# Gate and up weight sums of a seven-product FFN: subtractions on VectorE, or accumulating DMAs from DRAM

## The chip, the core and the metric

The kernel runs on one core of one Trainium2 chip. The metric is the device time of one execution in microseconds (us). The engines named below are PE (TensorE, matrix multiply), DVE (VectorE), ACT (ScalarE), POOL (GpSimd) and SP (SyncE, which here only issues DMAs). Each engine works through its own instructions in a fixed order, and an instruction that waits for a semaphore holds up everything behind it on the same engine.

## What is computed

A two-layer encoder trunk on 512 positions of width 1024, in float32. Layer 0 mixes by a gated linear recurrence (RG-LRU), layer 1 by stick-breaking attention; after each mixer comes a SwiGLU feed-forward block (FFN) with inner width 2816, and a last RMSNorm ends it.

```python
D_MODEL, SEQ, DEPTH, D_FF = 1024, 512, 2, 2816

def _swiglu(h, w_gate, w_up, w_down):
    g = h @ w_gate
    u = h @ w_up
    return (jax.nn.silu(g) * u) @ w_down

for layer in range(DEPTH):
    h = _rmsnorm(x, norm_mix_g[layer])
    x = x + (_rglru_mixer(h, ...) if layer % 2 == 0 else _sb_mixer(h, ...))
    h = _rmsnorm(x, norm_ffn_g[layer])
    x = x + _swiglu(h, ffn_w_gate[layer], ffn_w_up[layer], ffn_w_down[layer])
return _rmsnorm(x, final_g)
```

The change concerns the products with `w_gate` and `w_up` only (and the signs around them).

## The kernel before

**Float32 by three products.** Every weight block of 128x1024 floats is loaded by SP into an SBUF tile, then split: ACT casts it to a reduced float type (`wh`, line L236), and DVE or POOL subtracts that from the original to get the rest (`wl`, L237). PE multiplies high by high, low by high and high by low. One such loaded and split block is a "chunk". The method `chunk()` hands out chunks in the fixed order of the list made by `plan()`; in the FFN it keeps the splits three chunks ahead of PE and the loads up to eight ahead. In the FFN the split tiles have four buffers in turn (three `wh`/`wl`, and `wh4`/`wl4` for every fourth chunk), so the split of a chunk can begin only when PE is done with the chunk four places before it. Loads that go to `raw` tiles have four buffers.

**Seven products in place of eight.** In the FFN, the two halves of the positions and gate and up together form a 2x2 block product (rows: first and second 256 positions; columns: gate and up; the inner dimension cut in two halves of 512). It is done by a Strassen-Winograd scheme with seven block products, called q = 1 to 7 in the code. For this, the weights of one unit of 512 inner columns (units u = 0 to 4, two pieces c = 0, 1 for each product; unit 5 has 256 columns and one piece) come as four blocks: b0 (gate, first half of the inner dimension), b1 (up, first half), b2 (gate, second half), b3 (up, second half). The products take b0, b2 and b3 as they are, and four sums: q5 takes b1 - b0, q6 takes b3 - b1 + b0, q4 takes b2 - b3 + b1 - b0, and q7 takes b3 - b1.

**Where the sums are made.** The class `Piece` stands for one product's piece in the chunk list. `Piece.load()` issues the load of one block on SP (b0 and b2 into `raw` tiles, b1 and b3 into tiles `b1`, `b3` with two buffers each). `Piece.source()` is called when the chunk is split, and makes the sum by a DVE subtraction of 128x1024 floats (L76): into a tile `tt` for q5, in place for q6 and q4, and into b1's tile for q7. That is four subtractions for a piece, 11 pieces in a layer, so 88 in all.

**The order.** Unit 0 runs its products as 1, 2, 5, 6, 3, 7, 4, with no other chunk between them; its first four chunks (q1 and q2, both pieces) are loaded before the FFN begins, and its tiles for b1 and b3 lie in memory that the mixer before it holds until PE has done its last product. Units 1 to 5 run 1, 5, 6, 3, 7, 2, 4, with the down-projection's chunks (24 matmuls each, `down_pair`) of the unit before in between: in unit 1 the first of them stands behind q3, in later units behind q5. PE's order is written by hand; the order on the other engines is set by a scheduler that gives the splits a high priority. The splits of the down-projection's chunks put `wl` on POOL, those of the seven products on DVE. What PE leaves in its banks is added up by ACT copies (L684, L705, L712) and DVE additions (L689, L715, L723).

`ffn_in()` makes the seven products' left operands while the mixer's output projection still runs.

Of the kernel before, what the change touches and what calls it, by code (L numbers as in the profile page):

```python
# [52 lines left out]


class Piece:
    LOADS = {1: 0, 5: 1, 6: 3, 2: 2}
# [4 lines left out]
    def load(self):
        un, kern = self.unit, self.unit.kern
        n = self.LOADS.get(self.q)
        if n is None:
# [7 lines left out]
        kern.nc.sync.dma_start(t, un.src[n * un.np + self.c])

    def source(self):
        un, kern, q, c = self.unit, self.unit.kern, self.q, self.c
        sub = lambda o, x, y: kern.nc.vector.tensor_tensor(o, x, y, ALU.subtract)  # L76
        b = lambda n: un.b[n, c]
        if q == 1:
            return b(0)
        if q == 2:  # L80
            return b(2)
        if q == 3:
            return b(3)
# [12 lines left out]


class Kern:
# [232 lines left out]
    def ffn_in(self, m, g):  # L331
        nc = self.nc
        lo, hi = slice(0, HS), slice(HS, S)
        sub = lambda o, x, y: nc.vector.tensor_tensor(o, x, y, ALU.subtract)
# [7 lines left out]
        if m < 4:  # L342
            ua, w2 = self.tmp(), self.tmp()
            t, t3 = self.new("a11", F32R, first=True), self.new("s3", F32R, first=True)
# [266 lines left out]
    def ffn(self, l, gnext):  # L611
        nc, tc = self.nc, self.tc
        mm = nc.tensor.matmul
        with tc.tile_pool(name=f"ffn{l}", bufs=1) as self.fp, tc.manual_schedule(engines={mybir.EngineType.PE}):
# [50 lines left out]
                    mm(out, lhsT=w[1][:, ws], rhs=h[:, cs], start=False, stop=en, skip_group_check=True)  # L665

            def add(m, bank):
                nc.vector.tensor_tensor(self.x[m], self.x[m], bank, ALU.add)  # L668
# [511 lines left out]
```

## Time and profile before

| | |
|---|---|
| three timed runs | 1150.55, 1150.94, 1151.56 us (median 1150.94) |
| profiled execution, span from first to last instruction | 1150.0 us (its time beyond the span is not given apart) |
| PE busy | 1120.0 us, 97% of the span |
| DVE, ACT, POOL busy | 816.6, 647.0 and 298.3 us |
| mean granted TensorE clock | 0.990 of full speed |
| DMA | 114.23 MB, queue of SP 30.9% of 16 DMA engines' span |
| first FFN, PE's first product | 166.92 us from the start of the span |
| second FFN, PE's first product | 786.05 us |

How to read it: PE is busy nearly throughout, so an edit changes the time only where it lengthens or shortens a wait of PE, or PE's own work. The busy time of the other engines counts only through the moment at which they hand something to PE. Rows of the timeline show the start in us from the span's start, the duration, the engine, the line, and the tiles written and read; the bracket at a row's end is the idle time before it and what ended it.

### The profile page before, as it was taken

How to read it: one execution, taken by the hardware profiler on the slowest of the kernel's cores; microseconds unless marked ns; L12 is line 12 of the kernel's file. 1: busy time of each engine (PE TensorE's matmuls, PEld its weight loads, DVE VectorE, ACT ScalarE, POOL GpSimd, SP SyncE). 2: the span in 40 equal slices, each digit the busy share in tenths (PEclk: the TensorE clock that was granted, in tenths of full speed). 3: DMA queues.
4: the chain of work that ended last, by engine and by line, in shares of the span. 5: the costliest groups of instructions: out<-in, count | busy, mean ns of one | idle time of the engine just before them, and what ended most of it. 6: DMA issues, size and time to landing. Idle time of an engine off the chain costs nothing. (4 is left out here: it accounts for less than half of the span.)

```text
span 1150.0 us, 14308 instructions
## 1 busy us (share of the span) xinstructions
PE 1120.0 (97%) x5363; PEld 931.0 (81%) x5363; DVE 816.6 (71%) x1080; ACT 647.0 (56%) x967; POOL 298.3 (26%) x167
## 2 busy tenths in 40 slices
PE   8999999999999999999999999899999999999995
PEld 6887788888888888988888888778788888888884
DVE  7878889767574757473488888679967575765655
ACT  6598576634353444453489999767544434343442
POOL 2451333020111111272054444314011111101231
PEclk9999999999999999999999999899999999999997
DMA  7222234332424222122434334033432331322201
GB/s 241 91 90 91 96 105 169 96 114 79 134 74 134 68 92 92 58 89 94 118 95 117 92 90 108 25 109 111 147 128 92 95 120 61 117 84 92 74 19 74
DMA packets 35862, 114.23 MB, mean 99 GB/s; under 512 B 4560, under 2 KB 5584, under 8 KB 35792
## 3 DMA queue, kind: packets, MB, share of 16 engines
q1 hardware_dynamic: 35504, 112.66, 30.9%
q8 instruction: 42, 0.69, 0.2%
q10 hardware_dynamic: 288, 0.66, 0.2%
q14 instruction: 28, 0.23, 0.1%
HBM read 102.81 MB, written 2.10 MB: 91 GB/s over the span
## 5 line engine op out<-in xcount | busy, mean ns | idle before, releaser
L237 POOL TENSOR_TENSOR wl<-raw,wh 128x1024 fp32r<-128x1024 f32 (+1 forms) x74 | 177.9, 2405 | 642.2 <-ACT wh L236 638.5
L236 ACT CAST wh<-raw 128x1024 fp32r<-128x1024 f32 (+1 forms) x154 | 155.9, 1016 | 186.1 <-PE bank L644 88.2
L642 PE MATMUL bank<-wh,ow 128*128 128x512 f32 (+1 forms) x480 | 179.4, 374 | 3.6 <-DVE st L389 3.6
L644 PE MATMUL bank<-wh,ow 128*128 128x512 f32 (+1 forms) x480 | 178.3, 372 | 0.0
L643 PE MATMUL bank<-wl,ow 128*128 128x512 f32 (+1 forms) x480 | 178.3, 371 | 0.0
L237 DVE TENSOR_TENSOR wl<-raw,wh 128x1024 fp32r<-128x1024 f32 (+1 forms) x80 | 98.5, 1234 | 46.0 <-ACT wh L236 45.1
L236 ACT CAST wh<-tt 128x1024 fp32r<-128x1024 f32 x66 | 69.4, 1052 | 109.5 <-PE bank L664 55.1
L663 PE MATMUL bank<-hh,wh 128*128 128x512 f32 (+1 forms) x324 | 125.4, 387 | 0.0
L664 PE MATMUL bank<-hl,wh 128*128 128x512 f32 (+1 forms) x324 | 125.3, 387 | 0.0
L665 PE MATMUL bank<-hh,wl 128*128 128x512 f32 (+1 forms) x324 | 125.2, 387 | 0.0
L668 DVE TENSOR_TENSOR x<-x,bank 128x512 f32<-128x512 f32 x87 | 59.6, 685 | 85.2 <-PE bank L665 84.3
L642 PEld LDWEIGHTS bank<-wh,ow 128*128 128x128 f32 x480 | 90.4, 188 | 19.7 <-ACT wh L236 4.4
L237 DVE TENSOR_TENSOR wl<-tt,wh 128x1024 fp32r<-128x1024 f32 x66 | 80.6, 1222 | 34.9 <-ACT wh L236 34.5
L270 PE MATMUL bank<-uh,wh 128*128 128x512 f32 x256 | 102.4, 400 | 1.8 <-ACT wh L236 1.2
L644 PEld LDWEIGHTS bank<-wh,ow 128*128 128x128 f32 x480 | 90.4, 188 | 15.7
L643 PEld LDWEIGHTS bank<-wl,ow 128*128 128x128 f32 x480 | 90.5, 188 | 15.3
L272 PE MATMUL bank<-uh,wl 128*128 128x512 f32 x256 | 100.3, 392 | 1.4 <-DVE wl L237 1.4
L271 PE MATMUL bank<-ul,wh 128*128 128x512 f32 x256 | 99.7, 390 | 0.3 <-DVE ul L326 0.3
L237 DVE TENSOR_TENSOR wl<-b,wh 128x1024 fp32r<-128x1024 f32 x44 | 54.8, 1246 | 51.8 <-ACT wh L236 51.6
L236 ACT CAST wh<-b 128x1024 fp32r<-128x1024 f32 x44 | 46.3, 1053 | 62.1 <-PE bank L644 26.7
L665 PEld LDWEIGHTS bank<-hh,wl 128*128 128x128 f32 x324 | 60.8, 188 | 12.4
L663 PEld LDWEIGHTS bank<-hh,wh 128*128 128x128 f32 x324 | 60.9, 188 | 12.1
(219 smaller groups left out, 2422.3 us busy)
## 6 DMA issues: line engine op xcount, KB each, us to landing
raw<-w_gu SPq DMA_DIRECT2D x44, 512.0 KB, 3.5
b<-w_gu SPq DMA_DIRECT2D x44, 512.0 KB, 3.9
raw<-w_dn SPq DMA_DIRECT2D x44, 512.0 KB, 3.5
raw<-w_qk SPq DMA_DIRECT2D x16, 512.0 KB, 3.4
raw<-w_in SPq DMA_DIRECT2D x14, 512.0 KB, 3.7
raw<-w_ao SPq DMA_DIRECT2D x8, 512.0 KB, 3.8
raw<-w_v SPq DMA_DIRECT2D x8, 512.0 KB, 3.5
qh<-qx SPq DMA_DIRECT2D x32, 128.0 KB, 2.4
```

Of the source, the lines that this page charges most:

```text
L236: self.nc.scalar.copy(wh[:, c], raw[:, c])
L237: self.wl_engine(i).tensor_tensor(wl[:, c], raw[:, c], wh[:, c].bitcast(F32), ALU.subtract)
L270: mm(out, lhsT=wh, rhs=xh, start=first, stop=False)
L271: mm(out, lhsT=wh, rhs=xl, start=False, stop=False)
L272: mm(out, lhsT=wl, rhs=xh, start=False, stop=last)
L642: mm(out[j][:, :w], lhsT=oh[:, ts(j)], rhs=wh[:, ws], start=st, stop=False, skip_group_check=True)
L643: mm(out[j][:, :w], lhsT=oh[:, ts(j)], rhs=wl[:, ws], start=False, stop=False, skip_group_check=True)
L644: mm(out[j][:, :w], lhsT=ol[:, ts(j)], rhs=wh[:, ws], start=False, stop=en, skip_group_check=True)
L663: mm(out, lhsT=w[0][:, ws], rhs=h[:, cs], start=st, stop=False, skip_group_check=True)
L664: mm(out, lhsT=w[0][:, ws], rhs=lw[:, cs], start=False, stop=False, skip_group_check=True)
L665: mm(out, lhsT=w[1][:, ws], rhs=h[:, cs], start=False, stop=en, skip_group_check=True)
L668: nc.vector.tensor_tensor(self.x[m], self.x[m], bank, ALU.add)
```

## The change

The signs of the seven-product scheme are chosen so that all four weight sums are plain additions: q5 takes b0 + b1, q6 takes b0 + b1 + b3, q4 takes b0 + b1 + b3 + b2, and q7 takes b3 + b1. The left operands take the opposite signs where needed (`ffn_in`), and the FFN's result is subtracted from the residual in place of added.

The sums are no longer made by DVE. SP loads b0 a second time, into a tile `bu`, and b3 into a tile `bv` (two buffers each). POOL then issues DMAs that read a block from DRAM and add it into the tile: b1 into `bu` as soon as b0 has landed; b3 into `bu` once q5's split has read it; b2 into `bu` once q6's split has read it; b1 into `bv` once q3's split has read it. That is four accumulating DMAs of 512 KB for a piece, 88 in all. SP's loads stay 88 in number.

```diff
 class Piece:
-    LOADS = {1: 0, 5: 1, 6: 3, 2: 2}
+    LOADS = {1: ("raw", 0), 2: ("raw", 2), 5: ("bu", 0), 3: ("bv", 3)}
+    HOME = {1: 1, 2: 2, 5: 5, 6: 5, 4: 5, 3: 3, 7: 3}
+    NEXT = {5: 3, 6: 2, 3: 1}
...
+    def part(self, n):
+        return self.unit.src[n * self.unit.np + self.c]
+
+    def plus(self, n):
+        kern = self.unit.kern
+        kern.nc.gpsimd.dma_start(self.source(), self.part(n), accum_op=ALU.add)
+
     def load(self):
...
-        if n in (0, 2):
+        tag, n = self.LOADS[q]
+        if tag == "raw":
             t = kern.raw_buf()
         else:
             kern.tn += 1
-            t = kern.fp.tile([P, 1024], F32, tag=f"b{n}", bufs=2, name=f"b{n}_{kern.tn}")
-        un.b[n, self.c] = t
-        kern.nc.sync.dma_start(t, un.src[n * un.np + self.c])
+            t = kern.fp.tile([P, 1024], F32, tag=tag, bufs=2, name=f"{tag}_{kern.tn}")
+        un.b[q, self.c] = t
+        kern.nc.sync.dma_start(t, self.part(n))
+        if q == 5:
+            self.plus(1)
 
     def source(self):
...
-        if q == 7:
-            sub(b(1), b(3), b(1))
-            return b(1)
-        if q == 5:
...
-            sub(b("t"), b(1), b(0))
-        elif q == 6:
-            sub(b("t"), b(3), b("t"))
-        else:
-            sub(b("t"), b(2), b("t"))
-        return b("t")
+        return self.unit.b[self.HOME[self.q], self.c]
+
+    def after(self):
+        if self.q in self.NEXT:
+            self.plus(self.NEXT[self.q])
...
             self.split_piece(i, raw, wh, wl, slice(0, raw.shape[-1]))
+            if isinstance(e, Piece):
+                e.after()
...
-            nc.vector.tensor_tensor(w1[:, lo], ua[:, hi], ub[:, hi], ALU.add)
-            sub(w1[:, hi], w1[:, lo], ua[:, lo])
+            sub(w1[:, lo], ub[:, hi], ua[:, hi])
+            nc.vector.scalar_tensor_tensor(w1[:, hi], w1[:, lo], -1.0, ua[:, lo], ALU.mult, ALU.subtract)
...
-            sub(w2[:, hi], ub[:, lo], w1[:, hi])
+            nc.vector.scalar_tensor_tensor(w2[:, hi], ub[:, lo], -1.0, w1[:, hi], ALU.mult, ALU.subtract)
...
-            nc.vector.tensor_tensor(last[:, cs], last[:, cs], p[j][:, :HS], ALU.add)
+            nc.vector.tensor_tensor(last[:, cs], last[:, cs], p[j][:, :HS], ALU.subtract)
...
-                nc.vector.tensor_tensor(self.x[m], self.x[m], bank, ALU.add)
+                nc.vector.tensor_tensor(self.x[m], self.x[m], bank, ALU.subtract)
```

PE's 5343 program rows stand in the same order as before. Three places show what moves; the names are those of the tiles, with a running number, and the bracket lists the semaphores waited for (`DMAHW` is a transfer issued by SP, `DMASW` one issued by POOL).

DVE at the start of the first FFN, before: the sums of q5 and q6 (`tt_1545` and `tt_1563`, pieces 0 and 1) between the splits that use them (`wl_1548`, `wl_1566` for q5, `wl_1585`, `wl_1602` for q6).

```order
L76 TENSOR_TENSOR tt_1545<-b_190_1499,raw_1272 128x1024 [waits DMAHW7_49]
L237 TENSOR_TENSOR wl_1528<-raw_1434,wh_1527 128x1024 [waits DMAHW6_49,Activation_49]
L76 TENSOR_TENSOR tt_1563<-b_191_1501,raw_1326 128x1024 [waits DMAHW0_49]
L237 TENSOR_TENSOR wl_1548<-tt_1545,wh_1547 128x1024 [waits Activation_49]
L334 TENSOR_TENSOR ow_1470<-t_1463,ow_1469 128x512
L237 TENSOR_TENSOR wl_1566<-tt_1563,wh_1565 128x1024 [waits PE_49,Activation_49]
L334 TENSOR_TENSOR t_1464<-t_1462,t_1463 128x256
L76 TENSOR_TENSOR tt_1545<-b_192_1503,tt_1545 128x1024 [waits DMAHW1_49,DVE_49]
L334 TENSOR_TENSOR ow_1473<-t_1464,ow_1473 128x256 [waits Activation_49]
L76 TENSOR_TENSOR tt_1563<-b_193_1505,tt_1563 128x1024 [waits DMAHW2_49]
L237 TENSOR_TENSOR wl_1585<-tt_1545,wh_1584 128x1024 [waits Activation_49]
```

The same place of DVE in the change (`bu_1499` and `bu_1502` are pieces 0 and 1 of the sum, `bv_1513` is b3 of piece 0).

```order
L232 TENSOR_TENSOR wl_1528<-raw_1434,wh_1527 128x1024 [waits DMAHW6_49,Activation_49]
L331 TENSOR_TENSOR ow_1470<-t_1463,ow_1469 128x512
L331 TENSOR_TENSOR ow_1473<-t_1464,ow_1473 128x256 [waits Activation_49]
L232 TENSOR_TENSOR wl_1548<-bu_1499,wh_1547 128x1024 [waits DMASW0_49,Activation_49]
L232 TENSOR_TENSOR wl_1565<-bu_1502,wh_1564 128x1024 [waits DMASW1_49,PE_49,Activation_49]
L686 TENSOR_TENSOR r_1491<-r_1491,bank_74 128x512 [waits PE_49]
L686 TENSOR_TENSOR r_1492<-r_1492,bank_75 128x512 [waits PE_49]
L232 TENSOR_TENSOR wl_1584<-bu_1499,wh_1583 128x1024 [waits DMASW2_49,Activation_49]
L232 TENSOR_TENSOR wl_1620<-bv_1513,wh_1619 128x1024 [waits DMAHW3_49,Activation_49]
L232 TENSOR_TENSOR wl_1601<-bu_1502,wh_1600 128x1024 [waits DMASW3_49,Activation_49]
```

The four subtractions are gone, each split of q5 and q6 now waits for a transfer issued by POOL, and the split of q3's first piece (`wl_1620`) stands ahead of that of q6's second piece (`wl_1601`).

POOL at the same place, before: the last two additions of the norm's squares, and then the first splits of down-projection chunks.

```order
L380 TENSOR_TENSOR acc<-acc,t_1427 128x512 [waits Activation_49,Pool_49]
L380 TENSOR_TENSOR acc<-acc,t_1481 128x512 [waits Activation_49,Pool_49]
L237 TENSOR_TENSOR wl_1938<-raw_1795,wh_1937 128x1024 [waits DMAHW0_49,DVE_49,Activation_49]
L237 TENSOR_TENSOR wl_2006<-raw_1851,wh_2005 128x1024 [waits DMAHW2_49,DVE_49,Activation_49]
L237 TENSOR_TENSOR wl_2076<-raw_1941,wh_2075 128x1024 [waits DMAHW7_49,Activation_49]
```

And POOL there in the change.

```order
L377 TENSOR_TENSOR acc<-acc,t_1427 128x512 [waits Activation_49,Pool_49]
L68 DMA bu_1499<-w_gu 128x1024 [waits DMAHW1_49,PE_49]
L68 DMA bu_1502<-w_gu 128x1024 [waits DMAHW2_49]
L377 TENSOR_TENSOR acc<-acc,t_1481 128x512 [waits Activation_49,Pool_49]
L68 DMA bu_1499<-w_gu 128x1024 [waits DMASW0_49,DVE_49]
L68 DMA bu_1502<-w_gu 128x1024 [waits DMASW1_49,DVE_49]
L68 DMA bu_1499<-w_gu 128x1024 [waits DMASW2_49,DVE_49]
L68 DMA bv_1513<-w_gu 128x1024 [waits DMAHW3_49,DVE_49]
L68 DMA bu_1502<-w_gu 128x1024 [waits DMASW3_49,DVE_49]
L68 DMA bv_1531<-w_gu 128x1024 [waits DMAHW4_49,DVE_49]
L68 DMA bu_1663<-w_gu 128x1024 [waits DMAHW1_49,DMASW4_49,DVE_49]
```

Between the last norm addition and the first down-projection split POOL now issues the accumulating DMAs of unit 0; each waits for the transfer before it into the same tile and for DVE's split that reads that tile.

SP, loads at the start of the first FFN, before (`b_190`, `b_191` are b1 of the two pieces, `b_192`, `b_193` b3, `raw_1623` and `raw_1641` b0 of unit 1).

```order
L72 DMA b_190_1499<-w_gu 128x1024 [waits PE_49]
L72 DMA b_191_1501<-w_gu 128x1024
L72 DMA b_192_1503<-w_gu 128x1024
L72 DMA b_193_1505<-w_gu 128x1024
L72 DMA raw_1623<-w_gu 128x1024 [waits DMAHW3_49,DVE_49,Activation_49]
L72 DMA raw_1641<-w_gu 128x1024 [waits DMAHW4_49,DVE_49,Activation_49]
```

And SP there in the change.

```order
L81 DMA raw_1624<-w_gu 128x1024 [waits DMAHW3_49,DVE_49]
L81 DMA raw_1643<-w_gu 128x1024 [waits DMAHW4_49,DVE_49]
L81 DMA bu_1499<-w_gu 128x1024 [waits PE_49]
L81 DMA bu_1502<-w_gu 128x1024
L81 DMA bv_1513<-w_gu 128x1024
L81 DMA bv_1531<-w_gu 128x1024
L216 DMA raw_1794<-w_dn 128x1024 [waits DMAHW5_49,DVE_49]
L216 DMA raw_1849<-w_dn 128x1024 [waits DMAHW6_49,DVE_49]
L81 DMA bv_1751<-w_gu 128x1024 [waits DMAHW7_49,DMASW5_49,DVE_49]
L81 DMA bv_1769<-w_gu 128x1024 [waits DMAHW0_49,DMASW7_49,DVE_49]
L81 DMA bu_1663<-w_gu 128x1024 [waits DMAHW1_49,DMASW4_49,DVE_49]
```

The two loads of unit 1's b0 moved ahead of unit 0's four, because their buffers come free earlier; and the load of `bu_1663` (unit 1) now waits for the split of unit 0's q4, which reads the buffer last.

More of the change, by code (lines that the diff above doesn't have):

```diff
@@ L55 @@
 class Piece:
-    LOADS = {1: 0, 5: 1, 6: 3, 2: 2}
+    LOADS = {1: ("raw", 0), 2: ("raw", 2), 5: ("bu", 0), 3: ("bv", 3)}
+    HOME = {1: 1, 2: 2, 5: 5, 6: 5, 4: 5, 3: 3, 7: 3}
+    NEXT = {5: 3, 6: 2, 3: 1}
     def __init__(self, unit, q, c):
         self.unit, self.q, self.c = unit, q, c
+    def part(self, n):
[3 more added lines that the diff above has]
+        kern.nc.gpsimd.dma_start(self.source(), self.part(n), accum_op=ALU.add)
     def load(self):
-        un, kern = self.unit, self.unit.kern
-        n = self.LOADS.get(self.q)
-        if n is None:
+        un, kern, q = self.unit, self.unit.kern, self.q
+        if q not in self.LOADS:
             return
-        if n in (0, 2):
+        tag, n = self.LOADS[q]
+        if tag == "raw":
             t = kern.raw_buf()
@@ L69, in load @@
             kern.tn += 1
-            t = kern.fp.tile([P, 1024], F32, tag=f"b{n}", bufs=2, name=f"b{n}_{kern.tn}")
-        un.b[n, self.c] = t
-        kern.nc.sync.dma_start(t, un.src[n * un.np + self.c])
-    def source(self):
[L75 to L83, printed above, removed]
-        if q == 7:
-            sub(b(1), b(3), b(1))
-            return b(1)
-        if q == 5:
-            kern.tn += 1
-            un.b["t", c] = kern.fp.tile([P, 1024], F32, tag="tt", bufs=2, name=f"tt{kern.tn}")
-            sub(b("t"), b(1), b(0))
-        elif q == 6:
-            sub(b("t"), b(3), b("t"))
-        else:
-            sub(b("t"), b(2), b("t"))
-        return b("t")
+            t = kern.fp.tile([P, 1024], F32, tag=tag, bufs=2, name=f"{tag}_{kern.tn}")
[3 more added lines that the diff above has]
+            self.plus(1)
+    def source(self):
+        return self.unit.b[self.HOME[self.q], self.c]
+    def after(self):
+        if self.q in self.NEXT:
+            self.plus(self.NEXT[self.q])
 class Kern:
```

## The prediction

> **What bounds the kernel now.** I read the busy shares first, then what PE waited for, then the same by stage, and last the timeline around the places that the change touches. First row: busy us, share and instructions by engine. Next three: PE's largest waits (us in total, times, longest). Last four: stretches of the span, with busy us of PE, weight load, DVE, ACT, POOL, then granted clock, DMA share, GB/s.
>
> ```profile
> PE 1120.0 (97%) x5363; PEld 931.0 (81%) x5363; DVE 816.6 (71%) x1080; ACT 647.0 (56%) x967; POOL 298.3 (26%) x167
> ...
> PE bank L642 <- DVE st L389: 3.6, 2, 2.1
> PE bank L649 <- DVE x L668: 2.8, 8, 0.3
> PE bank L907 <- DVE awl L977: 2.7, 2, 2.3
> ...
> 167.00:205.00 38.00, 36.46 (x165) 30.02 (x164) 37.02 (x45) 25.24 (x33) 11.06 (x2) 1.00 0.54 182
> 205.00:490.00 285.00, 283.62 (x1368) 238.39 (x1367) 186.87 (x203) 124.89 (x155) 51.53 (x21) 1.00 0.29 94
> 790.00:840.00 50.00, 47.92 (x220) 39.58 (x219) 49.20 (x57) 32.08 (x41) 9.76 (x1) 1.00 0.40 135
> 840.00:1115.00 275.00, 273.62 (x1322) 229.97 (x1321) 175.52 (x190) 117.17 (x146) 54.26 (x22) 1.00 0.28 91
> ```
>
> PE bounds it. In the two FFNs (the four stretches) PE waits for DVE just 3.6 us at L642 and some 0.3 us at a time at L649. From 205 and from 840 on it misses 1.4 us of each stretch. Only in unit 0 of each FFN is DVE full too (37.02 of 38 us; 49.20 of 50). So the work taken from DVE has a ceiling of a few us of gain, while each new wait of PE counts whole.
>
> **What is removed.** The DVE subtractions of L76 (count | busy us, mean ns | idle before), and the place in unit 0 where DVE's lateness costs PE:
>
> ```profile
> L76 DVE TENSOR_TENSOR tt<-b,raw 128x1024 f32<-128x1024 f32 x22 | 30.7, 1395 | 0.5
> L76 DVE TENSOR_TENSOR tt<-raw,tt 128x1024 f32<-128x1024 f32 x22 | 26.8, 1217 | 0.2
> L76 DVE TENSOR_TENSOR tt<-b,tt 128x1024 f32<-128x1024 f32 x22 | 26.8, 1217 | 0.0
> L76 DVE TENSOR_TENSOR b<-b,b 128x1024 f32<-128x1024 f32 x22 | 26.6, 1217 | 0.2
> ...
> 200.28 0.39 PE L644 MATMUL bank<-wh,s 128*128 128x512 f32 x1
> 202.21 0.47 PE L642 MATMUL bank<-wh,ow 128*128 128x512 f32 x1 [1.54 <-DVE st L389]
> ...
> 201.39 0.67 DVE L723 TENSOR_TENSOR b<-b,bank 128x512 f32<-128x512 f32 x1
> ...
> 821.88 0.47 PE L642 MATMUL bank<-wh,ow 128*128 128x512 f32 x1 [2.08 <-DVE st L389]
> ```
>
> 88 subtractions, 110.9 us of DVE, go. Most stand beside PE's work and return nothing. What can return is the wait before q4 of unit 0: PE ends q7 at about 200.67 and needs the bank that DVE adds up at L723; DVE comes to it at 201.39, behind two subtractions of L76. A free DVE would start at once, and the addition's own 0.67 us stays, with 0.1 of handover: of 1.54 and 2.08 us some 0.8 each remain, so the gain is 0.7 + 1.3 = 2.0 us. Its bounds are 0 and 3.6.
>
> **What is added on the path.** An accumulating DMA now stands in the chain to four of seven splits, and POOL has none in this trace. Call L the time from POOL's reaching it to the data being usable. The nearest rows: size and median us from issue to landing of SP's transfers; the first two of the FFN's four loads, and all four; the fastest and slowest of that tile's loads; POOL's norm addition and its split (min/median/max ns; mean).
>
> ```profile
> b<-w_gu SPq DMA_DIRECT2D x44, 512.0 KB, 3.9
> raw<-w_dn SPq DMA_DIRECT2D x44, 512.0 KB, 3.5
> ...
> qh<-qx SPq DMA_DIRECT2D x32, 128.0 KB, 2.4
> ...
> b<-w_gu SPq DMA_DIRECT2D x2, 512.0 KB, 4.0
> ...
> b<-w_gu SPq DMA_DIRECT2D x4, 512.0 KB, 5.4
> ...
> DMA to landing us min/median/max: 3.4/3.9/7.2
> ...
> L380 POOL TENSOR_TENSOR acc<-acc,t x20: 1298/1424/9760, 137.0 to 796.7; 128x512 f32<-128x512 f32 x20
> ...
> L237 POOL TENSOR_TENSOR wl<-raw,wh 128x1024 fp32r<-128x1024 f32 x70 | 174.7, 2495 | 634.4 <-ACT wh L236 630.6 <-DVE qy L881 3.7
> ```
>
> Low end of L: 3.4, the fastest plain load (the addition free). High end: 7.2 + 9.76 = 17.0, the slowest load behind a POOL instruction stretched to its worst. I take 6.4: the median load 3.9; 1.5 for reading the tile as well, at the slope between 128 and 512 KB ((3.5 - 2.4) / 384 KB x 512 KB); and 1.0 for POOL, between nothing and its split's 2.5 (issuing is no pass over 512 KB, so nearer nothing). The value lies near the plain loads because the transfer is of their size and from the same DRAM.
>
> Of the 88, those count that nothing hides. **Unit 0** first:
>
> ```profile
> 166.92 0.39 PE L642 MATMUL bank<-wh,a 128*128 128x512 f32 x1
> ...
> 167.11 2.02 SPq L72 DMA_DIRECT2D b<-w_gu  x4
> ...
> 173.27 1.05 ACT L236 CAST wh<-tt 128x1024 fp32r<-128x1024 f32 x1
> ...
> 175.43 1.22 DVE L237 TENSOR_TENSOR wl<-tt,wh 128x1024 fp32r<-128x1024 f32 x1
> ...
> 177.80 0.39 PE L642 MATMUL bank<-wh,ow 128*128 128x512 f32 x1
> ```
>
> PE starts the FFN at 166.92, and q5 at 177.80 after four chunks of 2.72 us. The loads for q5 cannot go before 167.11, when PE leaves the memory. Before, q5's `wl` was done at 176.65, 1.15 us early. Now: b0 lands at 167.11 + 4.0 = 171.1; the first accumulation shares the DMA engines with three loads still under way, for which I add the 5.4 - 3.9 = 1.5 us that these loads themselves lost: 171.1 + 6.4 + 1.5 = 179.0; cast 1.05, `wl` 1.22 and 0.1 of handover, 2.4 in all: 181.4. PE waits 181.4 - 177.8 = 3.6 us. Next, b3 is added when that `wl` has read the tile: q6's first piece is ready 6.4 + 2.4 = 8.8 us after q5's start, where PE arrives after two chunks, 5.44: 3.4 us more. q6's second piece, q7 and q4 then follow within their time: q3 (5.44 us, no sum) lies between, and q7's sum starts some 1.2 us behind q6's split, is ready 1.2 + 6.4 + 2.4 = 10.0 after it, and is needed after four chunks, 10.9. So 7.0 us per FFN. The second FFN starts alike:
>
> ```profile
> 786.05 0.39 PE L642 MATMUL bank<-wh,a 128*128 128x512 f32 x1
> ...
> 786.24 1.75 SPq L72 DMA_DIRECT2D b<-w_gu  x4
> ...
> 794.91 1.22 DVE L237 TENSOR_TENSOR wl<-tt,wh 128x1024 fp32r<-128x1024 f32 x1
> ```
>
> **Unit 1** has q6 directly behind q5 too, and its `bu` loads wait for unit 0's q4 split, done at 195.5 before (194.31 below, plus 1.21). Counted from there without unit 0's delay, which moves both sides: load 3.9, L 6.4, split 2.4: q5 ready at 208.2, q6 at 217.0. PE comes to q6 at 219.43: 2.4 us to spare. **Units 2 to 5**, in the second FFN's rows: q4's `wl` ends at 869.65, load and L give 880.0, q5's cast comes at 883.88 anyway; q5's `wl` ends at 886.2, its sum is there at 892.6, q6's cast comes at 896.23. Nothing.
>
> ```profile
> 194.31 1.21 DVE L237 TENSOR_TENSOR wl<-tt,wh 128x1024 fp32r<-128x1024 f32 x1
> ...
> 219.43 0.48 PE L642 MATMUL bank<-wh,ow 128*128 128x512 f32 x1
> ...
> 868.42 1.23 DVE L237 TENSOR_TENSOR wl<-tt,wh 128x1024 fp32r<-128x1024 f32 x1 [0.23 <-ACT wh L236]
> ...
> 883.88 1.05 ACT L236 CAST wh<-tt 128x1024 fp32r<-128x1024 f32 x1 [0.72 <-PE bank L644]
> 884.96 1.23 DVE L237 TENSOR_TENSOR wl<-tt,wh 128x1024 fp32r<-128x1024 f32 x1 [0.80 <-ACT wh L236]
> ...
> 896.23 1.05 ACT L236 CAST wh<-tt 128x1024 fp32r<-128x1024 f32 x1 [0.83 <-PE bank L644]
> ```
>
> **Moved and minor.** Behind the waiting accumulations on POOL stand the last norm addition (1.4 us; its result is needed only after q3) and the down-projection splits, which stand three chunks ahead of PE; an issue of 1 us in front of them is covered. On DVE and ACT, what queues behind q5's waiting split is the copying out of q1 and q2, whose banks PE needs later. SP's early loads of unit 1's b0 go before 167.11, since their buffers come free with the splits of q1. The 16 operand instructions of another form (128x256) and the subtraction from the residual cost DVE what they did, to within 1 us, off PE's path. DMA traffic: 36 accumulations in units 1 to 5 are 18.9 MB a layer, against 26.8 MB at a share of 0.29 in the row from 205; at twice the cost per byte the share is 0.29 + 0.41 = 0.70, not the bound.
>
> **Sum.** 2 x 7.0 - 2.0 = +12.0 us on the profiled span of 1150.0: 1162.0. The median of the runs stands 0.9 above that span: 1163.
>
> **Rivals.**
> 1. The transfer is hidden anyway, and the freed DVE wins. The price falls by 2 us per FFN for each us of L (7.0 at 6.4), so with L at 3.4 a stall of 1.0 per FFN is left, and none if the first one shares no bandwidth either; the sum then lies between 2.0 - 2.0 = 0 and -3.6: 1147.3 to 1151. It decides for faster when L is under about 3. For it speaks that plain loads land in 3.4 to 3.9; against it, that the addition must read the tile too and POOL must issue it. The Trainium skill, "DMA: Bandwidth & Descriptors", section "Anatomy of one DMA — SWDGE (gpsimd) path", fits a DMA issued by GpSimd as 2.0 us plus bytes over 436 GB/s; for 512 KB an estimate by that page is 3.2 us, which is this rival; the trace here shows no DMA from POOL to hold it against.
> 2. The accumulation is slow, per transfer or per byte. At L = 10 unit 0 costs (10 - 2.8) + (10 - 3.0) = 14.2, q7's sum comes 2.7 late, and unit 1 becomes late by 2 x (10 - 6.4) - 2.4 = 4.8: 21.7 per FFN, 1150.9 + 43.4 - 2.0 = 1192. If a byte costs over 3.5 times a plain one, the DMA share passes 1 in units 1 to 5; at four times it would be 0.29 + 0.82 = 1.11, so 0.11 x 285 = 31 us more per FFN beyond unit 0's price. For it: POOL's norm addition took 9.76 us in unit 0, where it takes 1.3 elsewhere, so POOL can be held up when DVE is full. The Trainium skill, "SBUF — State Buffer", section "Who interferes with whom", says that a DVE instruction with two SBUF inputs contends with POOL's reads of SBUF, and infers that writing descriptors is not hit; the 9.76 agrees with the first, and no run here shows the second. Against it: with the sums gone DVE is no longer full there.
> 3. The middle case, L from 4.5 to 8: 1154 to 1175, the forecast's own range.
>
> **How the numbers follow.** The middle case has 0.53, with 1163 at its likeliest L. Rival 1 has 0.20, 0.11 of it faster than 1148.6 and 0.09 within 0.2% (2.3 us, about what a measurement of this kernel can tell from no change). Rival 2 has 0.24. The remaining 0.03 is a cover I do not see, time unchanged. So faster 0.11, same 0.12, slower 0.77. The range for 8 in 10 leaves out half of rival 1 below and the DMA-paced part of rival 2 above: 1149 to 1195.
>
> **What would show it.** After the change L76's rows are gone and DVE is busy some 705 us; a queue of 88 POOL-issued transfers appears, with 46 MB; PE's waits list two new ones per FFN, before q5 (to about 181.4) and before q6 of unit 0, for ACT's cast or DVE's `wl`, of 3 to 4 us each; the wait before q4 shrinks under 1 us; units 2 to 5 show no new wait. Wrong would be: no wait at q5 (L small), waits in every unit (transfers slow or DMA full), or late down-projection splits on POOL.

## The result, and the profile after

The changed kernel takes 1183.70 us (median of four runs, 1181.93 to 1186.44) against 1151.25 beside it on the same chip: a ratio of 1.0278, 95% interval 1.0261 to 1.0294, so 32.5 us more. The forecast was 12. The profiled execution is the slowest of the four (1186.44, span 1184.7).

The page of the profile, busy times first; then the DMA queues (packets, MB, share of 16 engines' time) and the DMA issues (median us from issue to landing); last what PE waited for.

```profile
PE 1133.9 (96%) x5363; PEld 935.1 (79%) x5363; DVE 719.9 (61%) x992; ACT 644.0 (54%) x967; POOL 355.8 (30%) x255
...
q1 hardware_dynamic: 35504, 112.66, 29.1%
q0 software_dynamic: 12672, 46.14, 22.6%
...
bu<-w_gu POOLq DMA_DIRECT2D x66, 512.0 KB, 5.5
...
bu<-w_gu SPq DMA_DIRECT2D x22, 512.0 KB, 4.3
...
PE bank L639 <- ACT wh L231: 10.8, 3, 5.4
PE bank L639 <- DVE b L720: 6.5, 2, 3.2
PE bank L640 <- DVE wl L232: 4.5, 8, 0.8
PE bank L660 <- DVE hl L650: 3.2, 2, 1.7
```

DVE lost 97 us of busy time (forecast 111). PE has new waits: for q5's cast (L639 for ACT's L231), for `wl`, and in unit 1 at the first down-projection (L660). Its wait for the bank that DVE adds up before q4 (L720) grew from 3.6 to 6.5 us. PE's busy time also rose by 13.9 us with the same 5363 matmuls, which the waits do not explain: 8.2 us of it lie in the two units 0 and 3.7 ahead of the first FFN. The stretches show why in unit 0 (PE, weight load, DVE, ACT, POOL busy, then granted clock, DMA share, GB/s):

```profile
169.29:185.43 16.14, 11.04 (x50) 8.82 (x48) 8.47 (x13) 8.26 (x14) 4.54 (x4) 0.96 0.96 282
185.43:190.00 4.57, 4.10 (x9) 2.92 (x10) 3.38 (x4) 1.04 (x1) 1.52 (x2) 0.50 0.39 49
...
230.00:290.00 60.00, 56.73 (x256) 45.22 (x255) 33.53 (x38) 26.38 (x34) 16.61 (x12) 1.00 0.74 180
290.00:500.00 210.00, 208.97 (x994) 174.83 (x993) 105.87 (x121) 88.77 (x111) 55.28 (x39) 1.00 0.64 154
```

Behind the wait at q5 PE runs at a granted clock of 0.50. From 290 on PE misses 1.03 us in 210, although the DMA engines are busy 0.64 of the time: units 2 to 5 cost nothing.

The timeline of the first FFN, one row of SP, POOL, ACT and PE each: q5's chain from the load of b0 through its accumulating DMA and its cast to PE.

```profile
169.47 0.81 SPq L81 DMA_DIRECT2D bu<-w_gu  x2
...
175.30 1.92 POOL L68 DMA_DIRECT2D bu<-w_gu  x2 [3.53 <-PE bank L641]
...
184.33 1.04 ACT L231 CAST wh<-bu 128x1024 fp32r<-128x1024 f32 x1 [7.40 <-DMA bu<-w_gu]
...
185.43 0.79 PE L639 MATMUL bank<-wh,ow 128*128 128x512 f32 x1 [5.11 <-ACT wh L231]
```

POOL reached the first accumulation 6.0 us after PE's first product (169.29), and it took 9.0 us to the cast.

For the rest one table, worked out from the timelines: where PE started the pieces of unit 0 (a and b), in us from the FFN's first product. The two rows of a kernel are the first and the second FFN. Before the change only q4 comes late.

```
kernel           q5a    q5b    q6a    q6b    q7a    q7b    q4a    q4b
before          10.88  13.60  16.32  19.04  28.02  30.87  35.29  38.11
                10.88  13.60  16.32  19.04  28.02  30.87  35.83  38.67
after           16.15  22.00  24.73  28.26  37.24  40.09  47.29  50.13
                16.41  21.56  24.79  28.72  37.70  40.55  47.65  52.06
fill            16.27  19.68  23.99  27.92  39.06  42.47  48.32  52.63
                16.48  20.35  24.81  29.87  40.27  45.21  49.51  52.35
plain           13.22  19.34  22.41  25.13  34.11  36.96  40.22  43.04
                13.44  19.56  22.78  25.50  34.48  37.33  40.58  43.41
u0_q5           13.52  19.05  21.77  24.49  33.47  36.32  43.99  49.25
                14.39  20.32  23.08  25.80  34.78  37.63  44.52  49.77
u0_q5only       12.25  16.24  19.51  22.23  32.04  34.89  38.26  41.07
                11.89  15.88  18.62  21.34  31.12  33.97  37.35  40.19
```

At q4b the changed kernel stands 12.0 us behind in the first FFN (50.13 less 38.11) and 13.4 in the second; unit 1 adds 4.6 and 2.3. Together that is 32.3, the loss between the medians (32.5). The two profiled spans lie 34.7 apart; the rest is mainly a later start of the first FFN (169.28 against 166.92 us), and in the other kernels' profiles that start varies from 165.95 to 169.72.

### The profile page after: what moved, and what is told of

Its sections match the earlier page's. It is cut to its first block, busy times and chain, and to the rows that moved or that the text cites. A ratio compares the mean times of both kernels' runs of the same rounds, so it can differ in the third digit from the quotient of the medians.

```text
span 1184.7 us, 14524 instructions
## 1 busy us (share of the span) xinstructions
PE 1133.9 (96%) x5363; PEld 935.1 (79%) x5363; DVE 719.9 (61%) x992; ACT 644.0 (54%) x967; POOL 355.8 (30%) x255
## 3 DMA queue, kind: packets, MB, share of 16 engines
q0 software_dynamic: 12672, 46.14, 22.6%
## 5 line engine op out<-in xcount | busy, mean ns | idle before, releaser
L231 ACT CAST wh<-raw 128x1024 fp32r<-128x1024 f32 (+1 forms) x154 | 155.9, 1016 | 173.5 <-PE bank L641 74.9
L639 PE MATMUL bank<-wh,ow 128*128 128x512 f32 (+1 forms) x480 | 182.3, 380 | 17.3 <-ACT wh L231 10.8
L640 PE MATMUL bank<-wl,ow 128*128 128x512 f32 (+1 forms) x480 | 181.3, 378 | 3.2 <-DVE wl L232 3.1
L641 PE MATMUL bank<-wh,ow 128*128 128x512 f32 (+1 forms) x480 | 180.1, 375 | 0.0
L68 POOL DMA_DIRECT2D bu<-w_gu x66 | 58.4, 885 | 323.8 <-DVE wl L232 156.9
L231 ACT CAST wh<-bu 128x1024 fp32r<-128x1024 f32 x66 | 69.2, 1051 | 157.2 <-DMA bu<-w_gu 77.2
L232 DVE TENSOR_TENSOR wl<-bu,wh 128x1024 fp32r<-128x1024 f32 x66 | 80.8, 1224 | 100.6 <-ACT wh L231 100.6
L660 PE MATMUL bank<-hh,wh 128*128 128x512 f32 (+1 forms) x324 | 125.7, 388 | 3.2 <-DVE hl L650 3.2
L639 PEld LDWEIGHTS bank<-wh,ow 128*128 128x128 f32 x480 | 91.7, 191 | 35.3 <-ACT wh L231 12.1
L641 PEld LDWEIGHTS bank<-wh,ow 128*128 128x128 f32 x480 | 91.7, 191 | 15.8
L232 DVE TENSOR_TENSOR wl<-bv,wh 128x1024 fp32r<-128x1024 f32 x44 | 53.9, 1224 | 81.4 <-ACT wh L231 81.4
L231 ACT CAST wh<-bv 128x1024 fp32r<-128x1024 f32 x44 | 46.3, 1052 | 75.2 <-PE bank L641 27.7
L660 PEld LDWEIGHTS bank<-hh,wh 128*128 128x128 f32 x324 | 60.9, 188 | 16.1 <-DVE hl L650 4.0
```

Source lines behind the costliest of these rows:

```text
L231: self.nc.scalar.copy(wh[:, c], raw[:, c])
L232: self.wl_engine(i).tensor_tensor(wl[:, c], raw[:, c], wh[:, c].bitcast(F32), ALU.subtract)
L639: mm(out[j][:, :w], lhsT=oh[:, ts(j)], rhs=wh[:, ws], start=st, stop=False, skip_group_check=True)
L640: mm(out[j][:, :w], lhsT=oh[:, ts(j)], rhs=wl[:, ws], start=False, stop=False, skip_group_check=True)
L641: mm(out[j][:, :w], lhsT=ol[:, ts(j)], rhs=wh[:, ws], start=False, stop=en, skip_group_check=True)
L660: mm(out, lhsT=w[0][:, ws], rhs=h[:, cs], start=st, stop=False, skip_group_check=True)
```

## The experiments

In all of them the signs are the new ones. Each says how the unit that it names makes its sums, and how the other units do: "dma" means that a unit's four sums are made as in the change, "dve" that they are made by DVE additions, with loads as before the change. The code shown is cut to the lines that matter.

**Signs, or transfers, and which unit.** `signs_dve`: all units dve. `u0_dve`: unit 0 dve, the rest dma. `u0_dma`: unit 0 dma, the rest dve.

```diff
+    MODE = {0: "dve"}        # u0_dve; u0_dma: {0: "dma"}; signs_dve: {}
+    DEFAULT = "dma"          # u0_dve; the other two: "dve"
...
+        self.mode = self.MODE.get(unit.u, self.DEFAULT)
...
+        if q == 5:
+            add(b("tt"), b("bu"), b(1))
+        elif q == 6:
+            add(b("tt"), b("bv"), b("tt"))
```

> The changed signs, with all sums made by DVE additions as before (no accumulating DMA). Every theory: about the time before, 1151 us (within 2 us), with PE's wait before q4 of unit 0 back at 1.5 to 2.1 us. If the 16 operand instructions of another form or the subtraction from the residual cost anything, it is 3 us or more above.

> Unit 0 of each FFN makes its sums on DVE, units 1 to 5 by accumulating DMAs (36 of 44 a layer). Theory chain (the loss is the serial chain of load, accumulation, split, accumulation at the start of an FFN, where PE has no lead): the 12 us of unit 0 in each FFN go, at most the 4.5 us of unit 1 stay: 1151 to 1160. Theory traffic (an accumulation costs the DMA engines twice a load, and all transfers come later for it): four fifths of the 32 us stay, about 1177.

> The reverse: only unit 0 sums by accumulating DMAs (8 of 44 a layer), units 1 to 5 on DVE. Theory chain: unit 0's 12 us in each FFN stay, 1172 to 1178. Theory traffic: a fifth of the 32 us, about 1157.

Measured: `signs_dve` 1151.82 us, ratio 1.0003 (0.9993 to 1.0012); `u0_dve` 1147.74, ratio 0.9965 (0.9953 to 0.9977); `u0_dma` 1183.01, ratio 1.0276 (1.0255 to 1.0297). The signs cost nothing. The 8 accumulations of unit 0 in each layer are enough for the whole loss; the other 36 a layer, without them, make the kernel a little faster. So it is not the traffic of all 88 that costs.

That `u0_dma` takes as long as the change does not mean that it loses its time in the same places. Unit 1 costs nothing there, and PE waits longer before q4: 6.28 and 5.68 us, against 3.21 and 3.25 in the change. In the first FFN DVE again had a first sum of unit 1 in front of the addition for q4, and that sum waited for its own load:

```profile
213.54 1.22 DVE L91 TENSOR_TENSOR tt<-bu,raw 128x1024 f32<-128x1024 f32 x1 [1.98 <-DMA bu<-w_gu]
...
216.72 0.77 PE L670 MATMUL bank<-wh,ow 128*128 128x512 f32 x1 [6.28 <-DVE b L751]
```

So the loss of unit 1 in the change needs both halves: a unit 0 that is late and a unit 1 that goes by DMA.

**The transfer alone.** `plain`: POOL's transfers as plain copies, everything else as in the change; the sums are left out of the result.

```diff
-        kern.nc.gpsimd.dma_start(self.source(), self.part(n), accum_op=ALU.add)
+        self.unit.kern.nc.gpsimd.dma_start(t, self.part(n))
```

> The changed kernel with POOL's 88 transfers as plain copies over the tile in place of additions (the sums are left out; queues, waits and bytes from DRAM stay). If the reading of the tile is what makes the chain long: a transfer takes 3.5 to 5 us in place of 5.5 to 9, the wait at q5 falls by 3 us or more, the DMA share in the later units falls from 0.65 to about 0.5, and the time to 1160 to 1170. If it is the chain as such and POOL's part in it: within 5 us of the changed kernel, 1179 to 1184.

Measured: 1162.66, ratio 1.0087 (1.0066 to 1.0109). Queue, landing, PE's first two waits, and two stretches behind them:

```profile
q0 software_dynamic: 12672, 46.14, 11.8%
...
bu<-w_gu POOLq DMA_DIRECT2D x66, 512.0 KB, 4.0
...
180.20 0.80 PE L670 MATMUL bank<-wh,ow 128*128 128x512 f32 x1 [2.18 <-ACT wh L262]
181.46 0.79 PE L671 MATMUL bank<-wl,ow 128*128 128x512 f32 x1 [0.47 <-DVE wl L263]
...
180.20:187.00 6.80, 6.33 (x14) 4.67 (x15) 4.04 (x5) 2.53 (x3) 1.10 (x2) 0.50 0.44 152
187.00:194.00 7.00, 7.00 (x32) 5.75 (x32) 4.39 (x4) 3.68 (x5) 2.11 (x4) 1.00 0.63 212
```

The addition makes the same 46.14 MB take 22.6% of the DMA engines' span in place of 11.8% (268 and 137 us of the span), 1.95 times the time, and lands in 5.5 us, not 4.0. The other 21 us of the loss hang on that. Even without it a wait of 2.18 us is followed by 6.8 us at half clock: q5's two pieces take 9.19 us (22.41 less 13.22) where 5.44 are needed. Of these 3.75 us, 1.0 is the wait for `wl` (the second row of PE starts 1.26 us behind the first, where 0.23 would do); 2.7 go with the half clock.

**Where the gain comes from.** `u1_dma`: only unit 1 dma, the rest dve.

```diff
+    MODE = {1: "dma"}
+    DEFAULT = "dve"
```

> The new signs; unit 1's four sums by accumulating DMAs, those of unit 0 and of units 2 to 5 by DVE additions. Theory 1 (the gain of the kernel with units 1 to 5 by DMA, 1147.7 against 1151.25, is the wait of PE before q4 of unit 0, where DVE stood behind the first sums of unit 1): almost the whole gain is here already, 1147.5 to 1149, and the wait of 1.8 us before q4 shrinks under 0.6 us. Theory 2 (the gain is that of a DVE with less to do in all the units): a fifth of it at most, 1150 to 1151.5, with the wait before q4 still above 1.5 us.

Measured: 1146.93, ratio 0.9962 (0.9949 to 0.9975); the wait before q4 is 0.42 us. Theory 1 holds for the waits. They account for 3.2 us between the two profiled executions; another 1.3 lie in the layer between the FFNs, where a stretch at half clock lasted 3.4 us in place of 6.8. DVE's timeline in `signs_dve`, and the row of PE that waits; L751 is the addition that PE needs for q4, and `tt<-bu,raw` are unit 1's first sums, which the scheduler put in front of it:

```profile
196.10 1.21 DVE L91 TENSOR_TENSOR tt<-bu,raw 128x1024 f32<-128x1024 f32 x1
...
198.71 1.23 DVE L91 TENSOR_TENSOR tt<-bu,raw 128x1024 f32<-128x1024 f32 x1
...
201.06 0.68 DVE L751 TENSOR_TENSOR b<-b,bank 128x512 f32<-128x512 f32 x1
...
201.89 0.47 PE L670 MATMUL bank<-wh,ow 128*128 128x512 f32 x1 [1.76 <-DVE st L417]
```

In `u0_dve` they are gone and the same addition starts earlier; PE's wait is what remains:

```profile
199.29 1.28 DVE L751 TENSOR_TENSOR b<-b,bank 128x512 f32<-128x512 f32 x2
...
200.12 0.47 PE L670 MATMUL bank<-wh,ow 128*128 128x512 f32 x1 [0.42 <-DVE b L751]
```

**Which of unit 0's sums can be moved.** `u0_mix`: in unit 0 DVE makes the sums of q5 and q6, accumulating DMAs those of q7 and q4, issued as soon as the splits of q5 and q6 have read the tiles; the rest dve. `best`: the same unit 0, the rest dma.

```diff
+        if self.mode == "mix":
+            if self.q == 5:
+                self.plus(b("bu"), 3)
+            if self.q == 6:
+                self.plus(b("tt"), 2)
```

> The new signs; in unit 0 the sums of q5 and q6 by DVE additions, those of q7 and q4 by accumulating DMAs into the tiles that the splits of q5 and q6 have read; units 1 to 5 by DVE additions. Theory 1 (an accumulation costs time only where its landing, 6 to 9 us, and the split of 2.4 us do not fit between the last reader and PE's need): q7's has about four chunks (11 us) and q4's about five, both fit, no new wait, and DVE has four additions less in unit 0, so the wait before q4 shrinks: 1148 to 1151. Theory 2 (accumulations in unit 0, where the DMA engines are full, delay everything around them, plain loads too): 1155 or more.

> The new signs; in unit 0 the sums of q5 and q6 by DVE and those of q7 and q4 by accumulating DMAs; units 1 to 5 all by accumulating DMAs. Theory 1 (only the two sums that PE meets at once, q5 and q6 of unit 0, must not go through a DMA): 1146.5 to 1148, since the kernel with units 1 to 5 by DMA measured 1147.7 and has waits of 0.4 us left before q4. Theory 2 (the accumulations of unit 0 then stand on POOL ahead of those of unit 1, and share the DMA engines with unit 1's loads, so unit 1's q5 comes late): 1150 to 1156, with a wait of PE at q5 or q6 of unit 1.

Measured: `u0_mix` 1149.05, ratio 0.9982 (0.9971 to 0.9993); `best` 1147.34, ratio 0.9962 (0.9948 to 0.9976). Four accumulations of unit 0 cost nothing where they have time; `best` gains no more than `u0_dve` or `u1_dma`, whose intervals it shares.

**The half clock in the changed kernel.** `fill`: the change, with matmuls on PE while it waits for q5.

```diff
+                if u == 0:
+                    oh = self.ops[0][1][0]
+                    for _ in range(FILL):      # 45
+                        mm(tb[1][:, :HS], lhsT=oh[:, :P], rhs=oh, start=True, stop=True, ...)
                 product(5, un, B, 0)
```

> The changed kernel, with 45 matmuls of 256 columns added on PE in front of q5 of unit 0 in each FFN, into a bank that nobody reads; by 0.113 us each they are about 5.1 us, as long as PE waits there (5.1 and 5.4 us), so PE's work goes on and its clock should stay at 1.00. Theory 1 (the half clock behind the wait is a cost of its own): the stretch of 4 to 5 us behind q5's start runs at full clock, PE saves 2 to 3 us in each FFN, and the time falls from 1183.7 to 1177 to 1180. Theory 2 (the chain of accumulations and splits sets the pace whatever PE's clock is: the next one can start only when the split before it has read the tile): PE comes earlier to q6 and waits there instead, 2.5 to 3.5 us in place of 0.8, and the time stays at 1182 to 1185.

Measured: 1187.16, ratio 1.0313 (1.0297 to 1.0328), so 3.5 us above the change's 1183.7, not below. The clock stayed at 1.00 behind q5, and q5b came at 19.68 in place of 22.00. But the lead was gone by q7 (39.06, not 37.24): PE waited 1.43 us at q6 and 2.02 us before q7's products. That is nearer to theory 2, though the time is 2 us above its range and the wait at q6 below its 2.5 to 3.5: the chain sets the pace, and in the changed kernel much of the half clock fills time that PE would have waited later.

**q5's sum alone, and q7's.** `u0_q5`: unit 0 makes q5's sum by the accumulating DMA, q7's too (into `bv` after q3's split, as in the change), q6's and q4's by DVE. `u0_q5only`: q7's also by DVE, out of q6's sum. The rest dve.

```diff
+            if q == 6:
+                add(b("tt"), b("bu"), b("bv"))
+                kern.nc.vector.tensor_tensor(b(1), b("tt"), b(1), ALU.subtract)  # u0_q5only
...
+        if self.mode == "q5" and self.q == 3:                                    # u0_q5
+            self.plus(b("bv"), 1)
```

> The new signs; in unit 0 only q5's sum is made by an accumulating DMA on the path (q7's by one far ahead of its need), q6's and q4's by DVE additions; units 1 to 5 by DVE. PE should wait for q5's cast 5.1 to 5.4 us in each FFN as in the changed kernel, and nothing paces q6 behind it. Theory 1 (half a clock for 6.8 us behind a wait costs 2.8 to 3.7 us where no chain stands behind it): 1151.5 + 2 x 5.2 + 2 x 3.3 = 1168.5, less up to 2 for q4's wait: 1166 to 1169. Theory 2 (the half clock costs nothing): 1160 to 1162. Theory 3 (q5's lateness alone makes the later waits at q7, q4 and in unit 1, through what queues on ACT and DVE): over 1175.

> As the kernel with q5's sum alone on the path, and q7's sum too made by DVE (q6's sum less b0, after q6's addition), so that unit 0 holds two accumulating DMAs in a layer, both for q5. There PE stood 5.5 and 6.7 us behind a schedule without waits at q6, and 9.9 and 10.4 at q4. Theory 1 (the second step came from q7's sum, issued only when q3's split has read its tile, and from what queues on ACT and DVE behind its split): no wait at q7, the wait at q4 under 2 us, and 1160 to 1163. Theory 2 (q5's lateness itself brings the wait at q4): 1168 to 1174 as before.

Measured: `u0_q5` 1172.46, ratio 1.0197 (1.0176 to 1.0217); `u0_q5only` 1156.01, ratio 1.0047 (1.0030 to 1.0063). The first missed all three ranges, the second came out below its best case. In `u0_q5` PE waits 2.48 and 3.35 us for q5's cast, not the 5.1 to 5.4 that were expected: SP's loads of down-projection chunks come later there, and the first accumulation took 6.1 and 6.7 us to the cast. Most of its loss lies further on. The rows of `u0_q5`: q7's second accumulation on POOL, the cast that waits for it on ACT, what stands behind that cast, DVE's addition for q4, and PE.

```profile
193.35 0.86 POOL L71 DMA_DIRECT2D bv<-w_gu  x1 [2.53 <-DVE wl L272]
...
200.93 1.05 ACT L271 CAST wh<-bv 128x1024 fp32r<-128x1024 f32 x1 [2.98 <-DMA bv<-w_gu]
201.88 1.99 ACT L271 CAST wh<-tt 128x1024 fp32r<-128x1024 f32 x2
203.90 1.28 ACT L422 ACT_TABLE_LOAD   x1
205.19 0.26 ACT L422 ACTIVATE st<-bank,eps 128x4 f32<-128x4 f32 x1
...
210.23 0.68 DVE L760 TENSOR_TENSOR b<-b,bank 128x512 f32<-128x512 f32 x1
...
211.05 0.77 PE L679 MATMUL bank<-wh,ow 128*128 128x512 f32 x1 [4.79 <-DVE st L426]
```

PE does not wait at q7 at all. It waits at q4, since ACT's queue (q4's casts, the load of a function table, the norm's root) stood behind the cast of q7, and DVE's queue behind ACT's. With q7's sum on DVE this wait is 0.49 us. So q7's two accumulations cost 4.3 and 3.5 us at q4 in the two FFNs (the steps from q7b to q4a), and 2.4 each from half a clock behind it. That is 12.6 of the 18.4 us between the two profiled spans (16.5 between the medians); another 5.1 had passed by q7b, most of it at q5. `u0_q5only`:

```profile
171.74 1.92 POOL L71 DMA_DIRECT2D bu<-w_gu  x2 [1.96 <-PE bank L680]
...
178.45 1.04 ACT L270 CAST wh<-bu 128x1024 fp32r<-128x1024 f32 x1 [3.51 <-DMA bu<-w_gu]
...
179.55 0.50 PE L678 MATMUL bank<-wh,ow 128*128 128x512 f32 x1 [1.21 <-ACT wh L270]
```

Here b0's block tile is kept for q7, so unit 1's b0 is not loaded ahead of unit 0's four blocks, and the down-projection's first blocks not beside the accumulation: POOL starts 4.4 us after PE's first product, not 6.0, and the first accumulation takes 6.7 us, not 9.0. PE's wait is 1.21 us, and the clock stays full behind it.

One more run belongs here, `u0_q5_fill`: `u0_q5` with the 45 matmuls of `fill` ahead of q5. If the half clock has a price of its own, 1160 to 1163 us were expected; if it has none, the time of `u0_q5` within 2 us. Measured: 1173.65, ratio 1.0206 (1.0189 to 1.0223), the time of `u0_q5`. The rows of PE are the fill, q5's first matmul and q6's first:

```profile
177.49 5.55 PE L742 MATMUL bank<-a 128*128 128x256 f32 x45
182.88 0.40 PE L680 MATMUL bank<-wh,ow 128*128 128x512 f32 x1
...
188.35 0.39 PE L680 MATMUL bank<-wh,ow 128*128 128x512 f32 x1
```

The clock was 1.00 throughout, and q5's two pieces took 5.47 us in both FFNs, where `u0_q5` needed 8.25 and 8.69. Of the 2.8 and 3.2 us between them 1.1 each is the wait for `wl`, so 1.7 and 2.1 go with the half clock. But the fill itself took 5.39 us where PE had waited 2.6 and 3.5, so PE came to q6 at 21.74 us in both FFNs, against 21.77 and 23.08 without it. The equal times therefore do not show that the half clock is free: the fill was too long and took the gain back.

**A fill of the right length.** `u0_q5only_fill`: `u0_q5only` with FILL = 24.

> The same with 24 matmuls of 256 columns (2.7 us) on PE in front of q5 of unit 0, into a bank that nobody reads: as long as PE waited there (2.5 and 3.4 us), not 5.1 as in the earlier try, which was twice the wait. Theory 1 (half a clock behind a wait costs 2 to 2.8 us where no chain paces PE): no stretch at 0.5 behind q5, and 4 to 5.5 us less than without the fill. Theory 2 (no price): within 1.5 us of it.

Measured: 1153.66, ratio 1.0028 (1.0017 to 1.0039), 2.3 us below `u0_q5only`, but the two intervals overlap, and the profiled spans are 1153.8 and 1153.1. That lies between the two theories. Since `u0_q5only` had no half clock left, this run says nothing of its price.

**Another order of the products.** `q3_first`: the change with q3, which needs no sum, ahead of q5 in unit 0. `q3_first2`: the same, with q7's accumulations kept behind q5's first two on POOL.

```diff
-        for q in ((1, 5, 6, 3, 7, 2, 4) if u else (1, 2, 5, 6, 3, 7, 4))
+        for q in ((1, 5, 6, 3, 7, 2, 4) if u else (1, 2, 3, 5, 6, 7, 4))
...
+                with un.kern.tc.issue_after(un.first.ins):      # q3_first2
+                    self.plus(b("bv"), 1)
```

> The changed kernel (all sums by accumulating DMAs) with unit 0's products in the order 1, 2, 3, 5, 6, 7, 4, so that q3, which needs no sum, gives the chain to q5 another 5.4 us. DVE makes two additions of 128x512 more in each FFN. Theory 1 (the chain of transfer and split paces unit 0): PE waits under 1 us before q5, but q6 stays at its time in the changed kernel, some 4 to 5 us after q5's end; q7's sum is ready early; q4 starts 7 to 10 us earlier than in the changed kernel, so 1163 to 1170. Theory 2 (the DMA engines, full in unit 0, set the pace whatever the order is): not under 1178.

> As the kernel with q3 ahead of q5, but on POOL q7's accumulations stand behind the first two of q5 (there they stood in front of them and waited for q3's splits, so q5's first accumulation was issued at 181.1 in place of 175.3). Theory 1 (unit 0 is paced by the chain of issue, transfer and split): q5's wait is 1 us or less, q6's 3 to 5, q4 starts about 9 us earlier than in the changed kernel, in all 1161 to 1170. Theory 2 (full DMA engines pace it): 1176 or more.

Measured: `q3_first` 1177.64, ratio 1.0246 (1.0228 to 1.0265); `q3_first2` 1172.52, ratio 1.0176 (1.0154 to 1.0198). The first lies between its two ranges, next to that of theory 2. POOL held q5's accumulation behind one that waited for q3's split:

```profile
178.27 1.01 POOL L71 DMA_DIRECT2D bv<-w_gu  x1 [6.05 <-DVE ow L362]
...
181.07 2.16 POOL L71 DMA_DIRECT2D bu<-w_gu  x2
...
190.81 0.80 PE L670 MATMUL bank<-wh,ow 128*128 128x512 f32 x1 [4.61 <-ACT wh L262]
```

In the second, q5's wait is down to 0.32 us, and the wait is now at q6, whose accumulation took 7.3 us (185.33 to 192.67), with half a clock behind it:

```profile
183.83 0.50 PE L674 MATMUL bank<-wh,ow 128*128 128x512 f32 x1 [0.32 <-ACT wh L266]
...
193.77 0.62 PE L674 MATMUL bank<-wh,ow 128*128 128x512 f32 x1 [3.18 <-ACT wh L266]
195.03 0.79 PE L675 MATMUL bank<-wl,ow 128*128 128x512 f32 x1 [0.64 <-DVE wl L267]
```

q4a came 3.8 and 3.1 us earlier than in the change, not 9: the time lies between the ranges of the two theories, 2.5 us above the first. The order helps, the chain through q6 stays.

## Why the prediction was wrong, step by step

The time lies in the stated range of 1149 to 1195, but only in the part that rival 2 brought in; the middle case ended at 1175. The direction, the place and the first link were right: PE waits at q5 for ACT's cast in both FFNs, units 2 to 5 show no new wait, and unit 0's accumulations alone are enough for the whole loss. The sum was 2 x 7.0 - 2.0 = 12. By the table, both FFNs together, it missed 8.5 us between q6b and q4b, 6.9 in unit 1, 3.6 at q5 and 1.3 between q5 and q6b: 20.3 us. The steps that failed, with the first FFN's numbers:

- **q5, 3.6 us: measured 5.3.** "b0 lands at 167.11 + 4.0" was wrong: POOL started 6.0 us after PE's first product, and the first accumulation took 9.0 us, not 7.9. The accumulation is long where two loads of down-projection chunks stand beside it: 8.6 to 9.0 us in the change and in `u0_dma`, 6.1 to 6.7 in `u0_q5` and `u0_q5only`, where these loads come later. For POOL's late start the step "SP's early loads of unit 1's b0 go before 167.11" is a candidate: without early loads (`u0_q5only`) it was 4.4 us, with them 4.9 (`plain`), 5.1 (`u0_dma`) and 6.3 (`u0_q5`). What makes that spread stays open. One small error went the other way: the wait ended with the cast, not with `wl`, which came as a wait of its own of 0.47 us.
- **q6, 3.4 us: measured 3.9** (9.22 less 5.3 at q6b), but only 0.8 us of it as waits at q6. The rest had passed at q5b, at half clock and in waits for `wl`. So the size came out nearly right, but not by the mechanism that was forecast. The L of 6.4 us was above the median landing of all accumulations (5.5), and too low for the first ones.
- **q7, "needed after four chunks, 10.9": wrong, the costliest step.** Its second accumulation was issued at 199.18, the fourth within 4 us, and the cast came at 208.16, 9.0 us later. PE itself hardly waited there. But ACT's and DVE's queues did, and the wait before q4, forecast to shrink from 1.5 to 0.8 us, grew to 3.21. These rows of the change show the same chain as in `u0_q5`:

```profile
199.18 0.86 POOL L68 DMA_DIRECT2D bv<-w_gu  x1 [0.57 <-DVE wl L232]
...
208.16 1.05 ACT L231 CAST wh<-bv 128x1024 fp32r<-128x1024 f32 x1 [2.95 <-DMA bv<-w_gu]
...
211.13 1.28 ACT L382 ACT_TABLE_LOAD   x1
...
215.74 1.28 DVE L720 TENSOR_TENSOR b<-b,bank 128x512 f32<-128x512 f32 x2
...
216.57 0.47 PE L639 MATMUL bank<-wh,ow 128*128 128x512 f32 x1 [3.21 <-DVE b L720]
```

  The prediction's sentence that what queues behind the waiting split is "the copying out of q1 and q2, whose banks PE needs later" looked at q5's split alone and not at q7's.
- **The gain of 2.0 us: the mechanism was right, and it was not there to be had.** What stood in DVE's way before q4 were unit 1's first sums; without them the kernel gains 0.38% (`u1_dma`), 4.4 us. Of this 3.2 us are these waits, inside the bound of 3.6; the rest lay outside the FFNs. In the changed kernel q7's lateness put a longer wait in the same place.
- **Unit 1, "2.4 us to spare": measured 4.6 and 2.3 us of loss.** From POOL's issue to the cast its first two accumulations took 8.1 and 9.8 us (rows below), where 6.4 were reckoned, and they start behind q4's split, late itself.

```profile
216.83 0.85 POOL L68 DMA_DIRECT2D bu<-w_gu  x1 [16.80 <-DVE b L720]
218.62 0.86 POOL L68 DMA_DIRECT2D bu<-w_gu  x1 [0.94 <-DMA bu<-w_gu]
...
224.97 1.05 ACT L231 CAST wh<-bu 128x1024 fp32r<-128x1024 f32 x1 [7.75 <-DMA bu<-w_gu]
...
228.45 1.05 ACT L231 CAST wh<-bu 128x1024 fp32r<-128x1024 f32 x1 [1.84 <-DMA bu<-w_gu]
```

- **Units 2 to 5 and the DMA share: right.** 0.70 was forecast, 0.64 to 0.74 was measured, without a wait.

Rival 2 (a slow accumulation, 1192 at L = 10) came nearest in time: the first accumulations of units 0 and 1 did take 8 to 10 us to the cast, though not the later ones. The Trainium skill's fit for a DMA issued by GpSimd ("DMA: Bandwidth & Descriptors", "Anatomy of one DMA — SWDGE (gpsimd) path"), which gave 3.2 us by estimate, is below the 4.0 us that a plain copy took here and well below the 5.5 of an accumulating one.

## What to carry to other kernels

For each sum that is to move into a DMA, write down the time between its tile's last reader and its need on the path, and compare it with issue, a landing under the traffic of that very moment (here 6.1 to 9.8 us from issue to split at the start of a stage; over the whole kernel the median landing is 5.5) and the split behind it; move only those that fit, as `u0_dve` and `best` do. Then ask of each engine that waits for the transfer, not of PE alone, what stands behind the waiting instruction: in `u0_q5` a cast that came 3 us late on ACT cost PE nothing at its own product, q7, and 4.3 us at the next, q4. And where an engine's relief gains time, look for the few instructions that stood in the way: here moving one unit's sums out of six gave as much as moving five units' (`u1_dma`, `u0_dve`).

## What the hardware showed that was not expected

**PE's half clock behind a short wait.** After waits of 2.18 and 2.40 us (`plain`), 2.48 and 3.35 us (`u0_q5`) and over 5 us (the change) the granted clock was 0.50 for 3.4 or 6.8 us; after the waits of 1.54 and 2.08 us of the kernel before, and of 1.21 us in `u0_q5only`, it stayed full. The length of the wait alone does not decide: behind 1.89 us (`signs_dve`, second FFN) the clock was 0.50 too, and behind 3.21 us (the change, q4 of the first FFN) it stayed 1.00, while behind 3.25 us at the same place of the second FFN it fell. At half clock the matmuls start every 0.43 us in place of 0.23. The price at q5, with the waits for `wl` taken out, was 1.7 and 2.1 us (`u0_q5` against `u0_q5_fill`) and 2.7 us (`plain`, first FFN, an estimate from its rows): from two thirds of the wait to a little more than it. No run here removed it and kept the gain in the total time. The Trainium skill, "TensorE: Matmul & The Clock Gate", "Part 1: The HAM clock gate", says that a free-running window of about 3.4 us is judged and that the clock halves after at least one idle window. The lengths of 3.4 and 6.8 agree; that 1.89 us of idleness were enough here does not.

**An accumulating DMA costs twice a plain one.** 1.95 times the DMA engines' time for the same bytes, and 5.5 us in place of 4.0 from issue to landing for 512 KB; POOL spends 0.86 us on each issue, and 0.53 on that of a plain copy (`plain`).
